# The mixers of the first block: the 16-row inverse moved ahead on VectorE, the convolution's input moved in front of it

## The chip, the cores and the metric

One core of a Trainium2 chip runs the whole program: two transformer-like blocks over 256 tokens of width 1024. Times are device microseconds (us) of one execution. The engines are TensorE (PE in the profile; its weight loads are PEld), VectorE (DVE), ScalarE (ACT), GpSimd (POOL) and SyncE (SP, which issues the weight loads). Each engine executes its instructions in a fixed order and waits on semaphores where an operand is not there yet.

## The reference, cut to what matters

The first block runs two layers; each has a mixer, then a feed-forward part (dense in the first layer, experts in the second). The change is in the mixer, which therefore runs twice. A mixer computes one input projection and three branches from it, and one output projection:

```python
proj = einsum('btd,de->bte', x, w_in)
(a_q, a_k, a_v, a_decay, a_beta, a_gate, c_glu, f_q, f_k, f_v, f_forget) = split_columns(proj, IN_SIZES)
# 1. gated delta rule, 6 heads of 64, chunks of 64 rows
qkv = silu(causal_depthwise_conv([a_q, a_k, a_v], gdn_conv_w))          # 4 taps
lower = where(strict, einsum('nbhcd,nbhsd->nbhcs', kb, kc) * decay, 0)
t_inv = triangular_solve(lower + eye, eye)                               # inverse of a 64 x 64 unit triangle
u, w = t_inv @ (vc * bc), t_inv @ (kb * exp(gc));  o_a = scan over 4 chunks, norm, gate
# 2. convolution
u = glu_a * sigmoid(glu_b);  u = causal_depthwise_conv(u, cnv_dw_w) + cnv_dw_b   # 31 taps, 256 channels
o_b = silu(layer_norm(u))
# 3. forgetting attention, 6 heads of 64, 256 tokens
o_c = softmax(q.k / 8 + decay, causal) @ v
mixed = [o_a, o_b, o_c] * mix_scale;  out = mixed @ w_out
```

## The kernel before, in words

The kernel is traced by one Python program (`Net.mixer1` for these mixers). The order in which statements are traced is their rank. A planner then lays every engine's instructions out in a fixed order ahead of time: whenever an engine is free in the planner's own timeline, the ready instruction of the best rank goes next, so an instruction of low rank fills a gap that one of high rank leaves while it is not ready. `with self.tc.issue_after(ins):` adds one more rule: what is traced inside it and runs on the engine of `ins` is placed behind `ins` on that engine. Only order is affected, and only that engine.

A projection is done in chunks of 256 columns, a 1 MB weight load each. `part` (L169 to L175) splits each half of a chunk into a rounded high part `wh` (ACT, L172) and the rest `wl` (DVE, L174), and `mm3` (L181) makes three matmuls of them, so a chunk is 48 matmuls of 128 x 128 by 256 columns and needs two ACT and two DVE instructions first. PSUM has two banks for projections (tag "a"), four for small work ("g") and two for the attention ("f").

The input projection has ten chunks in w_in_a (two tiles of 128 columns each, the last only one) and three in w_in_b. By `TILES_A`: chunks 0 to 2 are keys and queries of the delta rule, 3 the values v0 and v1, 4 v2 and f0, 5 f1 f2, 6 g0 g1, 7 g2 b0, 8 b1 a0, 9 a1, where f and g are the attention's keys and queries, b and a the two halves of the convolution's input.

A mixer is traced in this order (L624 to L636, L798):

- `pair_in`, `decays`, `pair_front` for chunks 0 to 2: 4-tap convolutions, norms, the triangles `NT`, and `lb`, the 16-row diagonal blocks of all twelve triangles.
- `spare(3)`, `spare(4)`: the values; `token_k`: keys by token.
- `emit(inverse(), scan(), fox(), conv(), gates())`, one after the other in rank. `inverse` begins with `invert16` (L503 to L513): 15 steps of a product (L509) and a reduction (L510) on DVE, each needing the one before, then a masking product (L511) and a 32 x 32 block transpose (L513). `invert32` goes from 16 to 64 rows by small matmuls, `solve` applies the inverse, `scan` carries the state over four chunks. `fox` projects chunks 5, 6, 7 and two of w_in_b, then does the attention for two blocks of 128 queries. `conv` projects chunks 8 and 9, gates the input into `up` (L748), does the last 6 (first mixer) or 8 (second) taps of each half of the channels with diagonal matrices on PE into one "a" bank (L757) and the other 25 or 23 one by one on DVE (L762, L764), adds both (L765) and normalises (L766 to L785). `gates` is the last chunk of w_in_b.
- the output projection, four chunks of w_out (L823).

Of the kernel before, what the change touches and what calls it, by code (L numbers as in the profile page):

```python
# [9 lines left out]
F32 = mybir.dt.float32  # L10
# [10 lines left out]
P = 128  # L21
D = 1024
KC = D // P
T = 256
# [53 lines left out]


TILES_A = "k0 q0 k1 q1 k2 q2 v0 v1 v2 f0 f1 f2 g0 g1 g2 b0 b1 a0 a1".split()  # L80
FOXC, GLUC = (5, 6, 7), (8, 9)

PCOLS1 = []
for _l in range(2):
# [19 lines left out]
class Net:  # L104
# [249 lines left out]
    def mixer1(self, l, x, xT):  # L354
        nc, A, ident = self.nc, self.A, self.ident
        V, S, PE = nc.vector, nc.scalar, nc.tensor
        wA, wB, wS = A["w_in_a"], A["w_in_b"], A["w_in_s"]
        mp = self.mp
        half = (slice(0, 64), slice(64, 128))

        def mm(out, lhsT, rhs, start=True, stop=True, **kw):
            PE.matmul(out, lhsT, rhs, start=bool(start), stop=bool(stop), skip_group_check=True, **kw)
# [28 lines left out]
        ps = self.ps("g", "cum").rearrange("p (t n) -> p t n", t=2)  # L391
# [68 lines left out]
        def pair_front(p):  # L460

            kq = kqs[p]
            sg = mp.tile([P, 2, T], F32, name="sg", bufs=3)
            S.activation(sg, kq, AF.Square)
            ps = self.ps("g", "l2")
            mm(ps, self.C["one64"], sg.rearrange("p a t -> p (a t)"))
            yield
            rs = mp.tile([P, 2, T], F32, name="sg", bufs=3)
            self.rsqrt(rs, ps.rearrange("p (a t) -> p a t", a=2), 1.0, 1e-6)
            V.tensor_tensor(kq, kq, rs, op=ALU.mult)  # L470
            yield
            at = AT[p] = mp.tile([P, 2, 2, 64], F32, name=f"AT{p}")
            nt = mp.tile([P, 2, 2, 64], F32, name=f"NT{p}")
            for o in range(2):
                e = E[2 * p + o]
                pk = self.ps("g", "kk")[:, :T].rearrange("p (t a n) -> p t a n", t=2, a=2)
                for t in range(2):
                    for c in range(2):
                        ts = slice(t * P + c * 64, t * P + c * 64 + 64)
                        mm(pk[half[c], t], kq[half[o], 0, ts], kq[half[o], :, ts])  # L480
                V.scalar_tensor_tensor(nt[:, o], pk[:, :, 0, :], -1.0, e[:, 1], op0=ALU.mult, op1=ALU.mult)
                V.scalar_tensor_tensor(at[:, o], pk[:, :, 1, :], 0.125, e[:, 0], op0=ALU.mult, op1=ALU.mult)
            n4 = NT[p] = nt.rearrange("p h t n -> p (h t) n")
            V.tensor_tensor(n4, n4, self.C["id64"][:, None, :].to_broadcast([P, 4, 64]), op=ALU.add)
            yield

            w = mp.tile([P, 4, 4, 16], F32, name="dgw")
            V.tensor_tensor(w, n4.rearrange("p i (b r) -> p i b r", b=4), self.C["in16"][:, None, :, None].to_broadcast([P, 4, 4, 16]), op=ALU.mult)
            d = mp.tile([P, 4, 16], F32, name="dg16", bufs=2)
            V.tensor_reduce(d, w.rearrange("p i b r -> p i r b"), axis=AX.X, op=ALU.add)  # L490
            yield
            for i in range(2):
                ex = mp.tile([P, 2, 16, 16], F32, name="sg", bufs=3)
                V.tensor_tensor(ex, d[:, 2 * i:2 * i + 2, :, None].to_broadcast([P, 2, 16, 16]),
                                self.C["id16"][:, None, None, :].to_broadcast([P, 2, 16, 16]), op=ALU.mult)
                pl = self.ps("g", "lb")
                mm(pl, self.C["one16"], ex.rearrange("p i r c -> p (i r c)"))
                S.activation(lb[:, 4 * p + 2 * i:4 * p + 2 * i + 2].rearrange("p i r c -> p (i r c)"), pl, AF.Copy)
            yield
# [3 lines left out]
        def invert16():  # L503

            xx = mp.tile([P, 12, 16], F32, name="x16")
            V.tensor_copy(xx, self.C["id16"][:, None, :].to_broadcast([P, 12, 16]))
            for r in range(1, 16):
                w = mp.tile([P, 12, 16], F32, name="w16", bufs=2)
                V.tensor_tensor(w[:, :, :r + 1], lb[:, :, r, :r + 1], xx[:, :, :r + 1], op=ALU.mult)  # L509
                V.tensor_reduce(xx[:, :, r], w[:, :, :r + 1], axis=AX.X, op=ALU.add)  # L510
            V.tensor_tensor(u32[:, 0].rearrange("p i (b r) -> p i b r", b=2), xx[:, :, None, :].to_broadcast([P, 12, 2, 16]),  # L511
                            self.C["even16"][:, None, :, None].to_broadcast([P, 12, 2, 16]), op=ALU.mult)
            V.transpose(u32[:, 1].rearrange("p i n -> p (i n)"), u32[:, 0].rearrange("p i n -> p (i n)"))  # L513

        def invert32(p):
            u, n4 = u32[:, :, 4 * p:4 * p + 4], NT[p]
# [95 lines left out]
        def spare(c):  # L612

            names = TILES_A[2 * c:2 * c + 2]
            ps = self.proj_a(wA[l, c][:, :1024 * len(names)], xT, tiles=len(names))
            for i, n in enumerate(names):
                if n[0] == "v":
                    value(ps[:, i, :], int(n[1]))
                else:
                    S.activation({"b": glu[:, 0:2], "a": glu[:, 2:4], "f": foxqk[:, 0:3], "g": foxqk[:, 3:6]}[n[0]][:, int(n[1]), :],  # L620
                                 ps[:, i, :], AF.Copy)
# [4 lines left out]
        for p in range(3):  # L626
            decays(p)
        self.weave(*(pair_front(p) for p in range(3)))
        spare(3)
        spare(4)  # L630
        for p in range(3):
            token_k(p)

        def fox():

# [50 lines left out]
                yield  # L686

        def inverse():
            invert16()
            yield  # L690
            self.weave(*(invert32(p) for p in range(3)))
            for p in range(3):
                solve(p)
                yield
# [42 lines left out]

        cv, csq = mp.tile([P, 2, T], F32, name="ccv"), glu[:, 0:2, :]

        def conv():  # L740

            for c in GLUC:
                spare(c)
            sg = glu[:, 0:2, :]
            self.sigmoid(sg, sg)
            up = mp.tile([P, 2, 30 + T], F32, name="cup")
            V.memset(up[:, :, 0:30], 0.0)
            V.tensor_tensor(up[:, :, 30:], glu[:, 2:4, :], sg, op=ALU.mult)  # L748
            yield
            near = 31 - (6, 8)[l]  # L750
            dw, db = self.col1(f"dww{l}"), self.col1(f"dwb{l}")
            pc = self.ps("a", "conv").rearrange("p (c n) -> p c n", c=2)
            for c in range(2):
                for j in range(near, 31):
                    dg = mp.tile([P, P], F32, name="dgt", bufs=2)
                    S.activation(dg, ident, AF.Copy, scale=dw[:, c * 31 + j:c * 31 + j + 1])
                    mm(pc[:, c, :], dg, up[:, c, j:j + T], start=j == near, stop=j == 30)  # L757
            for c in range(2):
                for j in range(near):
                    w = dw[:, c * 31 + j:c * 31 + j + 1]  # L760
                    if j == 0:
                        V.tensor_scalar(cv[:, c, :], up[:, c, 0:T], w, db[:, c:c + 1], op0=ALU.mult, op1=ALU.add)  # L762
                    else:
                        V.scalar_tensor_tensor(cv[:, c, :], up[:, c, j:j + T], w, cv[:, c, :], op0=ALU.mult, op1=ALU.add)  # L764
            V.tensor_tensor(cv, cv, pc, op=ALU.add)  # L765
            yield  # L766
            ps = self.ps("f", "cmean")
            for c in range(2):
                mm(ps[:, :T], self.ones, cv[:, c, :], start=c == 0, stop=c == 1)
            for c in range(2):  # L770
                V.scalar_tensor_tensor(cv[:, c, :], ps[:, :T], -1.0 / 256, cv[:, c, :], op0=ALU.mult, op1=ALU.add)
            S.activation(csq, cv, AF.Square)
            ps = self.ps("f", "cvar")
            for c in range(2):
                mm(ps[:, :T], self.ones, csq[:, c, :], start=c == 0, stop=c == 1)
            crs = glu[:, 2, :]
            self.rsqrt(crs, ps[:, :T], 1.0 / 256, 1e-5)
            lg_, lb_ = self.col1(f"clg{l}"), self.col1(f"clb{l}")
            for c in range(2):
                V.tensor_tensor(cv[:, c, :], cv[:, c, :], crs, op=ALU.mult)  # L780
                V.tensor_scalar(cv[:, c, :], cv[:, c, :], lg_[:, c:c + 1], lb_[:, c:c + 1], op0=ALU.mult, op1=ALU.add)
            V.tensor_scalar(csq, cv, -40.0, None, op0=ALU.max)
            self.sigmoid(csq, csq)
            V.tensor_tensor(cv, cv, csq, op=ALU.mult)
            yield  # L785
# [9 lines left out]
        msc = mp.tile([P, 8], F32, name="msc")  # L795
        V.tensor_copy(msc, self.col1(f"mix{l}"))
        V.tensor_scalar(msc[:, 0:3], msc[:, 0:3], self.col1(f"gnw{l}"), None, op0=ALU.mult)
        self.emit(inverse(), scan(), fox(), conv(), gates())  # L798
        mT = self.new_xT()
        for c in range(2):  # L800
            g = msc[:, 3 + c:4 + c]
# [1112 lines left out]
```

## Time and profile before

| | us |
|---|---|
| median of three timed runs (lowest, highest) | 2173.09 (2165.69, 2177.9) |
| the profiled execution | 2177.81 |
| its span | 2176.0 |
| PE busy in the span | 2079.3 |
| DVE busy | 1295.8 |
| ACT busy | 1017.1 |
| first mixer's output projection, last matmul | 203.0 |
| second mixer's | 608.6 |

The profile gives, for one execution, every instruction with its engine, line, tiles and times. A busy PE is modelled and includes matmuls at half clock, so the granted clock is read beside it. An engine's idle time stands in brackets behind the wait's releaser.

### The profile page before, as it was taken

How to read it: one execution, taken by the hardware profiler on the slowest of the kernel's cores; microseconds unless marked ns; L12 is line 12 of the kernel's file. 1: busy time of each engine (PE TensorE's matmuls, PEld its weight loads, DVE VectorE, ACT ScalarE, POOL GpSimd, SP SyncE). 2: the span in 40 equal slices, each digit the busy share in tenths (PEclk: the TensorE clock that was granted, in tenths of full speed). 3: DMA queues.
4: the chain of work that ended last, by engine and by line, in shares of the span. 5: the costliest groups of instructions: out<-in, count | busy, mean ns of one | idle time of the engine just before them, and what ended most of it. 6: DMA issues, size and time to landing. Idle time of an engine off the chain costs nothing. (4 is left out here: it accounts for less than half of the span.)

```text
span 2176.0 us, 31850 instructions
## 1 busy us (share of the span) xinstructions
PE 2079.3 (96%) x12770; PEld 1598.7 (73%) x12770; DVE 1295.8 (60%) x1903; ACT 1017.1 (47%) x1445; POOL 12.7 (1%) x27
## 2 busy tenths in 40 slices
PE   8998999899979999999999999999899999999998
PEld 7887999778766565565565565555699988888997
DVE  6767955676666555454564465454555568765444
ACT  6545444464435454444454454443444444644443
POOL 0000000000000000000000000000000000000000
PEclk9979999998889999999999999999999999999999
DMA  6313675422359999999999999999455553444552
GB/s 236 104 44 118 213 258 182 137 90 96 139 178 347 364 406 378 415 415 371 401 372 383 400 389 393 421 417 398 168 192 180 190 183 126 136 164 155 186 183 98
DMA packets 78987, 545.36 MB, mean 251 GB/s; under 512 B 8960, under 2 KB 11272, under 8 KB 13936
## 3 DMA queue, kind: packets, MB, share of 16 engines
q1 hardware_dynamic: 76112, 527.40, 63.8%
q0 software_dynamic: 2720, 15.84, 2.0%
q8 instruction: 103, 1.69, 0.3%
q14 instruction: 52, 0.43, 0.1%
HBM read 536.72 MB, written 6.49 MB: 250 GB/s over the span
## 5 line engine op out<-in xcount | busy, mean ns | idle before, releaser
L174 DVE TENSOR_TENSOR wl<-raw,wh 128x1024 fp32r<-128x1024 f32 (+1 forms) x662 | 798.1, 1217 | 432.3 <-ACT wh L172 420.5
L172 ACT ACTIVATE wh<-raw 128x1024 fp32r<-128x1024 f32 (+1 forms) x662 | 690.7, 1054 | 627.9 <-PE a_pA L184 270.3
L183 PE MATMUL a_pA<-xTh,wh 128*128 128x256 f32 x1456 | 419.0, 289 | 6.2 <-ACT foxqk L620 3.5
L185 PE MATMUL a_pA<-xTh,wl 128*128 128x256 f32 x1456 | 415.5, 286 | 0.8 <-DVE wl L174 0.7
L184 PE MATMUL a_pA<-xTl,wh 128*128 128x256 f32 x1456 | 415.6, 286 | 0.4 <-DVE xTl L278 0.2
L183 PEld LDWEIGHTS a_pA<-xTh,wh 128*128 128x128 f32 x1456 | 280.8, 193 | 14.7 <-ACT foxqk L620 5.6
L184 PEld LDWEIGHTS a_pA<-xTl,wh 128*128 128x128 f32 x1456 | 281.0, 193 | 5.3 <-issue 3.2
L185 PEld LDWEIGHTS a_pA<-xTh,wl 128*128 128x128 f32 x1456 | 280.8, 193 | 3.8 <-issue 2.2
L1033 PE MATMUL a_up<-raw,xef 128*64 128x512 f32 x896 | 213.5, 596 | 0.0
L184 PE MATMUL a_up<-wl,xeh 128*128 128x512 f32 x448 | 180.7, 403 | 0.5 <-DVE wl L174 0.4
L183 PE MATMUL a_up<-wh,xeh 128*128 128x512 f32 x448 | 177.7, 400 | 0.0
L185 PE MATMUL a_up<-wh,xel 128*128 128x512 f32 x448 | 177.3, 396 | 0.0
L1033 PEld LDWEIGHTS a_up<-raw,xef 128*64 128x64 f32 x896 | 65.1, 137 | 127.8 <-issue 122.3
L1038 DVE TENSOR_TENSOR mos<-mos,a_up 128x512 f32<-128x512 f32 x42 | 28.8, 685 | 200.3 <-PE a_up L1033 149.8
L183 PE MATMUL a_pB<-wh,xTh 128*128 128x256 f32 x480 | 141.5, 296 | 5.7 <-ACT glu L620 3.2
L185 PE MATMUL a_pB<-wh,xTl 128*128 128x256 f32 x480 | 138.6, 291 | 1.6 <-DVE xTl L278 1.6
L184 PE MATMUL a_pB<-wl,xTh 128*128 128x256 f32 x480 | 139.8, 292 | 0.0
L1066 PE MATMUL y_y<-raw,mof 128*64 128x512 f32 x448 | 132.8, 602 | 0.7 <-ACT mof L1052 0.7
L184 PEld LDWEIGHTS a_up<-wl,xeh 128*128 128x128 f32 x448 | 84.6, 189 | 34.5 <-issue 11.4
L183 PEld LDWEIGHTS a_up<-wh,xeh 128*128 128x128 f32 x448 | 84.7, 189 | 28.1 <-ACT wh L172 7.3
L185 PE MATMUL acc_acc<-wh,ffl 128*128 128x512 f32 x264 | 102.0, 392 | 0.0
L184 PE MATMUL acc_acc<-wl,ffh 128*128 128x512 f32 x264 | 101.9, 392 | 0.0
(556 smaller groups left out, 2703.2 us busy)
## 6 DMA issues: line engine op xcount, KB each, us to landing
raw<-in_moe_w_dram SPq DMA_DIRECT2D x336, 1024.0 KB, 9.2
raw<-in_ffn_in_dram SPq DMA_DIRECT2D x44, 1024.0 KB, 4.9
raw<-in_ffn_w_dram SPq DMA_DIRECT2D x33, 1024.0 KB, 5.0
raw<-in_w_in_a_dram SPq DMA_DIRECT2D x24, 1024.0 KB, 4.9
raw<-in_ffn_out_dram SPq DMA_DIRECT2D x22, 1024.0 KB, 4.9
raw<-in_w_out_dram SPq DMA_DIRECT2D x12, 1024.0 KB, 4.9
raw<-in_w_in_g_dram SPq DMA_DIRECT2D x12, 1024.0 KB, 4.9
raw<-in_w_in_b_dram SPq DMA_DIRECT2D x6, 1024.0 KB, 5.1
```

Source lines behind the costliest of these rows:

```text
L172: nc.scalar.activation(wh[:, :m], raw[:, o:o + m], AF.Copy)
L174: nc.vector.tensor_tensor(wl[:, :m], raw[:, o:o + m], wh[:, :m].bitcast(F32), op=ALU.subtract)
L183: mm(out, lh, rh, start=start, stop=False, skip_group_check=True)
L184: mm(out, lh, rl, start=False, stop=False, skip_group_check=True)
L185: mm(out, ll, rh, start=False, stop=stop, skip_group_check=True)
L1033: PE.matmul(ps[r], xe[0][:, k0, r], w[:, k * 512:k * 512 + 512], start=k0 == 0, stop=k0 == 7, skip_group_check=True)
L1038: V.tensor_tensor(s, s, pp[1], op=ALU.mult)
L1066: PE.matmul(py[h][r], hf[:, k, r], w[:, j * 1024 + h * 512:j * 1024 + h * 512 + 512], start=b == 0 and k == 0, stop=b == 6 and k == 3, ski ...
```

## The change

`invert16` is traced right after `pair_front`, ahead of the values' chunks and of token_k, and returns its last instruction, `solved`. Chunks 7, 8 and 9 are traced in front of the woven block, chunks 5 and 6 stay in the attention. The whole `emit` stands inside `issue_after(solved.ins)`. The convolution is cut in two: `conv_in` (gating and the diagonals on PE) comes behind the scan and ahead of the attention, the taps on DVE stay behind the attention. The convolution's mean and variance use a PSUM bank of tag "g" in place of "f".

```diff
-FOXC, GLUC = (5, 6, 7), (8, 9)
+GLUC, FOXC = (7, 8, 9), (5, 6)
...
-            V.transpose(u32[:, 1].rearrange("p i n -> p (i n)"), u32[:, 0].rearrange("p i n -> p (i n)"))
+            return V.transpose(u32[:, 1].rearrange("p i n -> p (i n)"), u32[:, 0].rearrange("p i n -> p (i n)"))
...
         self.weave(*(pair_front(p) for p in range(3)))
+        solved = invert16()
         spare(3)
         spare(4)
         for p in range(3):
             token_k(p)
+        for c in GLUC:
+            spare(c)
...
         def inverse():
-            invert16()
-            yield
             self.weave(*(invert32(p) for p in range(3)))
...
-        def conv():
-
-            for c in GLUC:
-                spare(c)
+        up = mp.tile([P, 2, 30 + T], F32, name="cup")
+
+        near = 31 - (6, 8)[l]
+        dw, db = self.col1(f"dww{l}"), self.col1(f"dwb{l}")
+        pc = self.ps("a", "conv").rearrange("p (c n) -> p c n", c=2)
+
+        def conv_in():
+
             sg = glu[:, 0:2, :]
             self.sigmoid(sg, sg)
-            up = mp.tile([P, 2, 30 + T], F32, name="cup")
             V.memset(up[:, :, 0:30], 0.0)
             V.tensor_tensor(up[:, :, 30:], glu[:, 2:4, :], sg, op=ALU.mult)
-            yield
...
                     dg = mp.tile([P, P], F32, name="dgt", bufs=2)
                     S.activation(dg, ident, AF.Copy, scale=dw[:, c * 31 + j:c * 31 + j + 1])
                     mm(pc[:, c, :], dg, up[:, c, j:j + T], start=j == near, stop=j == 30)
+            yield
+
+        def conv():
+
             for c in range(2):
                 for j in range(near):
...
-            ps = self.ps("f", "cmean")
+            ps = self.ps("g", "cmean")
...
-            ps = self.ps("f", "cvar")
+            ps = self.ps("g", "cvar")
...
-        self.emit(inverse(), scan(), fox(), conv(), gates())
+        with self.tc.issue_after(solved.ins):
+            self.emit(inverse(), scan(), conv_in(), fox(), conv(), gates())
```

## Rows read from the trace of the kernel before

**Rows 1.** The page's 40 slices of the span: PE's busy tenths, granted clock in tenths.

```profile
PE   8998999899979999999999999999899999999998
PEclk9979999998889999999999999999999999999999
```

**Rows 2.** Windows, first mixer: stretch and length, each engine's busy time, PEclk, DMA share, GB/s.

```profile
87.70:122.60 34.90, 34.85 (x485) 31.47 (x486) 25.87 (x67) 17.29 (x41) 0.00 (x0) 0.99 0.41 141
122.60:146.60 24.00, 24.00 (x187) 16.50 (x183) 12.50 (x38) 8.93 (x33) 0.00 (x0) 0.51 0.01 2
146.60:165.00 18.40, 18.32 (x180) 16.62 (x176) 15.70 (x36) 8.09 (x16) 0.00 (x0) 1.00 0.17 58
165.00:184.00 19.00, 13.84 (x80) 11.85 (x80) 14.33 (x36) 10.50 (x24) 2.06 (x4) 0.82 0.30 115
```

**Rows 3.** Windows, second mixer's stretch at half clock.

```profile
525.40:552.70 27.30, 27.30 (x210) 19.26 (x210) 14.00 (x41) 10.40 (x36) 0.00 (x0) 0.51 0.00 1
```

**Rows 4.** Timeline of PE, first mixer: start, duration, line, tiles, count, idle before.

```profile
87.75 0.39 PE L183 MATMUL a_pB<-wh,xTh 128*128 128x256 f32 x1 [1.58 <-ACT glu L620]
...
165.83 1.13 PE L362 MATMUL f_cmean<-ccv,ones 128*128 128x256 f32 x4 [0.81 <-DVE ccv L765]
...
174.49 0.66 PE L267 MATMUL g_tr<-call,mixed 128*128 128x128 f32 x4 [1.39 <-DVE mixed L816]
...
202.61 0.28 PE L184 MATMUL a_pB<-wl,xTh 128*128 128x256 f32 x1
202.73 0.28 PE L185 MATMUL a_pB<-wh,xTl 128*128 128x256 f32 x1
207.14 2.21 PE L869 MATMUL a_tr<-call,x 128*128 128x128 f32 x9 [4.13 <-DVE x L864]
```

**Rows 5.** Timeline of DVE, first mixer.

```profile
81.38 0.18 DVE L509 TENSOR_TENSOR w<-lb,x 128x24 f32<-128x24 f32 x1 [1.00 <-ACT lb L498]
...
88.98 0.26 DVE L509 TENSOR_TENSOR w<-lb,x 128x96 f32<-128x96 f32 x1
89.27 0.25 DVE L510 TENSOR_REDUCE x<-w 128x12 f32<-128x96 f32 x1
...
106.73 0.58 DVE L513 STREAM_TRANSPOSE u<-u 128x384 f32<-128x384 f32 x1
...
165.10 0.67 DVE L765 TENSOR_TENSOR ccv<-ccv,a_conv 128x512 f32<-128x512 f32 x1
```

**Rows 6.** Groups by line on DVE, 81.3 to 107.4 us.

```profile
L174 DVE TENSOR_TENSOR wl<-raw,wh 128x1024 fp32r<-128x1024 f32 x6 | 7.3, 1223 | 1.2 <-ACT wh L172 1.2
L509 DVE TENSOR_TENSOR w<-lb,x 128x24 f32<-128x24 f32 (+14 forms) x15 | 4.0, 268 | 1.2 <-ACT lb L498 1.0
L510 DVE TENSOR_REDUCE x<-w 128x12 f32<-128x24 f32 (+14 forms) x15 | 3.9, 262 | 0.2
...
L560 DVE TENSOR_TENSOR kbg<-g_ktok,ce 128x256 f32<-128x256 f32 x3 | 1.2, 414 | 0.0
```

**Rows 7.** Timeline of ACT: copies of chunk 6 and of chunk 7's gated half.

```profile
79.03 0.65 ACT L620 ACTIVATE foxqk<-a_pA 128x256 f32<-128x256 f32 x2
...
87.32 0.38 ACT L620 ACTIVATE glu<-a_pA 128x256 f32<-128x256 f32 x1
```

**Rows 8.** Windows: the start after PE's stop behind the first output projection.

```profile
207.10:211.10 4.00, 3.94 (x18) 3.58 (x18) 3.62 (x13) 2.57 (x6) 0.00 (x0) 0.57 0.00 0
```

**Rows 9.** Groups by line on DVE, 118 to 166 us: taps, and the attention's reductions.

```profile
L764 DVE SCALAR_TENSOR_TENSOR ccv<-cup,p,ccv 128x256 f32<-128x256 f32 x48 | 20.6, 476 | 0.2
...
L661 DVE TENSOR_REDUCE fsx<-f_fl 128x2 f32<-128x512 f32 (+1 forms) x4 | 2.2, 558 | 11.7 <-PE f_fl L362 11.7
```

**Rows 10.** Timeline of DVE, second mixer: the chain's first link and its transpose.

```profile
484.22 0.18 DVE L509 TENSOR_TENSOR w<-lb,x 128x24 f32<-128x24 f32 x1 [1.00 <-ACT lb L498]
...
509.57 0.58 DVE L513 STREAM_TRANSPOSE u<-u 128x384 f32<-128x384 f32 x1
```

**Rows 11.** Timeline of PE, second mixer: the output projection's last matmul.

```profile
608.33 0.28 PE L185 MATMUL a_pB<-wh,xTl 128*128 128x256 f32 x1
```

More of the change, by code (lines that the diff above doesn't have):

```diff
@@ L738, in mixer1 @@
         cv, csq = mp.tile([P, 2, T], F32, name="ccv"), glu[:, 0:2, :]
-        def conv():
-            for c in GLUC:
-                spare(c)
+        up = mp.tile([P, 2, 30 + T], F32, name="cup")
[3 more added lines that the diff above has]
+        def conv_in():
             sg = glu[:, 0:2, :]
             self.sigmoid(sg, sg)
-            up = mp.tile([P, 2, 30 + T], F32, name="cup")
             V.memset(up[:, :, 0:30], 0.0)
             V.tensor_tensor(up[:, :, 30:], glu[:, 2:4, :], sg, op=ALU.mult)
-            yield
-            near = 31 - (6, 8)[l]
-            dw, db = self.col1(f"dww{l}"), self.col1(f"dwb{l}")
-            pc = self.ps("a", "conv").rearrange("p (c n) -> p c n", c=2)
             for c in range(2):
```

## The prediction

> **What bounds the kernel now.** I read the page's slices first: TensorE (PE) is at 0.9 or above nearly everywhere, and its granted clock dips in the slices of the two mixers of the first block [rows 1]. Next, the windows of the first of them. From 87.7 to 165.0 us PE never stands still (34.85 of 34.90, 24.00 of 24.00 and 18.32 of 18.40 us busy), but from 122.6 to 146.6 it runs at 0.51, the lower level of 1.2 GHz [rows 2]. The second mixer does the same for 27.3 us [rows 3]. Then the timeline of PE: the output projection ends at 202.73 + 0.28 = 203.0 us [rows 4]. Its 4 x 48 matmuls follow each other every 0.12 us (two neighbours in [rows 4]), so it is worth 23.0 us and stands as if it had begun at 180.0. Between 165.0 and 180.0 lie only nine small pieces of PE work, from the 1.13 us of cmean to the 0.66 us of the last transposes, 7.0 us by their durations [rows 4]: 8 us of that tail are waits. Last, VectorE (DVE): the inverse's chain runs from 81.38 to 107.31 us [rows 5].
>
> So a mixer has three reserves: 12.0 us (half of 24.0) of lost clock, 8 us of waits in the tail, and whatever PE could do earlier. The profiled execution took 2177.81 us for a span of 2176.0; the median of the three timed runs is 2173.09, 4.7 less. I work with differences from the profiled one and subtract them from the median.
>
> **The change, part by part.**
>
> **1. The inverse is done earlier.** Its 15 products and 15 reductions last 4.0 and 3.9 us [rows 6]; alone, each follows 0.03 to 0.04 us after the end of the one before (89.27 after 88.98 + 0.26 [rows 5]), so 30 x 0.035 = 1.0 us is added, and 1.1 us for the masking product and the transpose (0.55 and 0.58): 10 us. It took 26, because weight splits (six of 1.22 us in that stretch), token work and the attention's reductions were placed between its links [rows 6]. Now everything of the woven block waits behind the transpose on DVE; what is still allowed between are operations traced before it: three products and three scalings of the values, three taps of v2, six of token_k (the splits of chunks 3 to 9 are through by then: chunk 9's one stands where chunk 7's first stood, at 79 us). These 15 cost about 0.41 us each, as token_k's [rows 6], but each fills a link's own gap, so I add 0.25 each: 3.5 us. The start stays at 81.38, since what feeds it is unchanged. Solved at 81.4 + 10 + 3.5 = 95.0 us; bounds 91.5 (nothing between) and 100 (all 15 in full, some beyond that). It was 107.3.
>
> **2. The price: PE has nothing to do meanwhile.** The splits of the attention's chunks are DVE work of the woven block, so they are queued behind the transpose too. ScalarE's halves are not, but PE needs both. Before, five chunks fed PE until it waited at 86.2 (1.58 us, released by the copy of the gated input [rows 4]): the v chunks 3 and 4, then 5 and 6 (6 copied out at 79.03) and 7 (its gated half at 87.32) [rows 7]. Now 7, 8, 9 stand in the place of 5, 6, 7, and chunk 9 has one tile: 24 x 0.12 = 2.9 us less work. PE is out of projections at 86.2 - 2.9 = 83.3 us and gets the next at 95. In between it has the transposes of v2 and k, 0.95 us (an estimate from their share around 94 us). About 11 us idle, where it was 1.5.
>
> After such a stop the clock is down: when PE had waited 4.13 us before 207.14, the next 4 us ran at 0.57 [rows 4, 8], a loss of 4.0 x 0.43 = 1.7 us. The Trainium skill, "TensorE: Matmul & The Clock Gate", section "Why this matters for your kernels", says to leave no idle gaps between bursts of matmuls, because the clock then falls to half; it speaks against this wait, and the row agrees. [...]
>
> **3. What then runs beside what.** After the transpose the small matmuls (three 32-row inverses, solve, scan, the convolution's diagonals) rank first, and five chunks of 5.8 us (chunks 5 and 6 and three of w_in_b) lie under them as filling. Before, four and a half of these lay ahead and only one was left beside the small work; there the engine did 18-, 32- and 64-row matmuls when the clock fell at 122.6. With dense 128-row chunks mixed in I expect most of the 12.0 us back. What is left is the end of the attention, which now comes after its late chunks with only w_in_b's last chunk beside it. Lost clock after the change: 4 us (1.7 at the restart, the rest there); bounds 0 and 14 (the clock stays down for another 24 us).
>
> **4. The convolution.** No instruction is added or removed: still 31 taps for each of two channel groups, on PE (the last 6 or 8 of each) and DVE. The input gating moves from the back to 95 us (the DVE product waits for the transpose), the diagonals follow. The first mixer's last 48 taps on DVE are 20.6 us, and DVE then sat idle 11.7 us in front of the attention's reductions with taps queued behind them [rows 9]. They ended so late that the sum of the two halves stood at 165.10 [rows 5], and the chain behind it (mean, variance, sigmoid, splits) held the output projection. Now the taps can start 25 us earlier; between 95 and 150 us DVE has about 30 us of other work (ten splits of 1.22 us [rows 6]; the inverse, scan and attention some 17, an estimate from the timeline) and 20 of taps, so the sum should come by 150 and the chain be covered. Waits left in the tail: 3 us, for the attention's last output and its transposes; bounds 0 and 8 (as now). The move of its mean to another PSUM tag is costed at nothing, since no wait of PE names a bank there.
>
> The diagonals' accumulator now holds one of two projection banks from 95 us until the sum. With one bank each chunk waits for its copy, 1.58 us in the row at 87.75 [rows 4], five times: 8 us if nothing else is ready. I take 0, because small work is: the half-clock stretch alone holds 12 us of it at full clock [rows 2], and the scan comes on top. 8 stays as a bound.
>
> DMA: the weight loads change their order on SP's queue, not their number; none is added on POOL's.
>
> **Sum for the first mixer**, in PE time at full clock: 165.0 - 87.7 = 77.3, less 12.0 of lost clock = 65.3; plus 2.9 (the tile that is now behind), less 0.95 done in the wait, plus 7.0 of the tail. 95.0 + 65.3 + 2.9 - 0.95 + 7.0 = 169.2, against 180.0: 10.8 us of room, minus 4 of clock and 3 of waits = 3.8 us gained. The second mixer's chain starts at 484.22 and ends at 510.15 [rows 10], the same 25.9 us; its output projection ends at 608.61 [rows 11]. Its half-clock stretch is 3.3 us longer, its tail about as much shorter, so I take the same: 7.6 in all. 2173.1 - 7.6 = **2166 us** (2170 for a profiled execution like this one). Its own range: 2158 to 2172.
>
> **The rivals.**
>
> A. *The tail and the clock come back whole.* For it: waits on DVE and half clock were each other's cause (a reduction waiting for a slow PE holds the taps [rows 9]). Then clock loss 1.7, waits 1: 10.8 - 2.7 = 8.1 a mixer, and 3.5 more if solved comes at 91.5; 16 to 23 in all, **2154**. Against it: the 11 us stop.
>
> B. *It does not do what it says:* wherever a chain link is not ready, the planner still puts something between, so solved comes at 100, PE stands 16 us, and what is gained behind is given back in front. Room 5.8, minus 4 and 3: -1.2 a mixer, **2175**.
>
> C. *The stop breaks the clock and the small work keeps it down.* One mechanism: PE stands idle from 83 us, restarts low, and what ranks first is the 32- and 64-row work that before the change ran 24 us at 0.51 [rows 2]. For it: exactly that work could not bring the clock back then. Against it: chunk 5 can enter as soon as its split of 1.22 us is done. Price: lost clock 12 + 1.7, waits 3: 10.8 - 16.7 = -6 a mixer, **2185**. It decides from about 8 us of lost clock a mixer, above which the kernel is slower than before.
>
> D. *One bank.* Four of the five copies are not covered, 6 us: 3.8 - 6 = -2.2 a mixer, **2177**. For it: the wait at 87.75, when chunk 4 held the other bank; against it: there no small work was ready.
>
> **How the numbers follow.** Forecast 0.42, A 0.20, B 0.13, C 0.17, D 0.08. About 0.5% (10.9 us) is what a measurement of this kernel can tell from no change. Faster by more: A and nearly two fifths of the forecast's case, 0.36. Within it: the rest of the forecast's, B and D, 0.44. Slower: C and a few of D, 0.20. The range for eight in ten runs from a little beyond A to C: 2149 to 2186.
>
> **What would show it.** Right: DVE's transpose (L513) near 95 and 498 us, with no weight split between the chain's links; PE's wait ahead of the first chunk after it about 11 us long; the granted clock near 1.0 from about 100 to 140 us; the convolution's sum (L765) before 155; the output projection of the first mixer ending near 199. Wrong: splits still between the links, or the transpose after 100 (B); a half-clock stretch of 15 us or more behind it (C); PE waiting on ACT copies at every chunk (D). Outside the mixers every stage should keep its length within 1 us; if time moves there, the forecast's ground is wrong.

## The result and the profile after

The changed kernel takes 2188.66 us (median of five, 2188.06 to 2188.87) against 2173.09 (2165.69 to 2177.9): ratio 1.0071, 95% interval 1.0049 to 1.0092. It is slower; 2166 was forecast. The profiled execution took 2188.06 us, its span is 2186.3.

Profile after, DVE's timeline in the first mixer: the chain's first link and its transpose, and the convolution's sum.

```profile
81.16 0.18 DVE L509 TENSOR_TENSOR w<-lb,x 128x24 f32<-128x24 f32 x1 [1.34 <-ACT lb L498]
...
94.87 0.58 DVE L513 STREAM_TRANSPOSE u<-u 128x384 f32<-128x384 f32 x1
...
128.47 0.69 DVE L769 TENSOR_TENSOR ccv<-ccv,a_conv 128x512 f32<-128x512 f32 x1
```

The inverse is there 11.9 us earlier and the sum 36.6 us earlier than in [rows 5]. In the second mixer the transpose starts at 504.23, where [rows 10] had 509.57, though that mixer began 6.2 us later. Beside the chain's links stand only values and keys, no weight split (groups on DVE, 81 to 95.5 us; columns as in [rows 6]):

```profile
L509 DVE TENSOR_TENSOR w<-lb,x 128x24 f32<-128x24 f32 (+14 forms) x15 | 4.0, 268 | 1.6 <-ACT lb L498 1.3
L510 DVE TENSOR_REDUCE x<-w 128x12 f32<-128x24 f32 (+14 forms) x15 | 4.0, 265 | 0.4
L425 DVE SCALAR_TENSOR_TENSOR v<-a_pA,p,v 128x255 f32<-128x255 f32 (+2 forms) x3 | 1.4, 479 | 0.0
L560 DVE TENSOR_TENSOR kbg<-g_ktok,ce 128x256 f32<-128x256 f32 x3 | 1.2, 414 | 0.0
...
```

PE's waits from 80 to 209 us (what waits, for what, us in total, times, longest):

```profile
PE g_x L362 <- DVE u L513: 7.3, 1, 7.3
PE g_vtok L573 <- DVE v L570: 3.1, 1, 3.1
PE f_fl L362 <- ACT fp L668: 2.5, 1, 2.5
PE f_fpt L677 <- ACT fpT L679: 1.5, 1, 1.5
PE a_pA L183 <- ACT glu L620: 0.9, 1, 0.9
PE a_conv L362 <- DVE cup L752: 0.9, 1, 0.9
PE f_fo L362 <- ACT fpT L679: 0.4, 1, 0.4
```

The first two, 10.4 us, are PE's stop ahead of the transpose. Windows of the first mixer, and of the second mixer's two low stretches (length, then busy PE, PEld, DVE, ACT, POOL; PEclk; DMA):

```profile
83.20:95.60 12.40, 1.97 (x14) 1.36 (x14) 11.37 (x39) 3.01 (x7) 0.00 (x0) 0.67 0.00 1
95.60:101.10 5.50, 4.60 (x107) 4.14 (x108) 5.44 (x10) 0.81 (x2) 0.00 (x0) 0.51 0.01 3
101.10:165.90 64.80, 62.81 (x724) 55.01 (x723) 44.98 (x106) 31.96 (x75) 0.00 (x0) 1.00 0.29 99
165.90:183.00 17.10, 14.61 (x48) 9.93 (x49) 9.84 (x26) 7.84 (x26) 0.53 (x1) 0.50 0.11 45
183.00:208.60 25.60, 25.60 (x217) 25.43 (x215) 16.33 (x29) 11.72 (x17) 1.54 (x3) 1.00 0.51 179
496.90:510.60 13.70, 5.30 (x111) 4.46 (x110) 13.19 (x34) 0.81 (x2) 0.00 (x0) 0.50 0.04 6
575.40:589.10 13.70, 12.78 (x37) 7.78 (x37) 8.54 (x24) 7.80 (x25) 0.54 (x1) 0.50 0.08 27
```

The 24.0 us at half clock of [rows 2] are gone: from 101.1 to 165.9 the clock is whole. In their place stand the stop with its restart, and 17.1 us at half clock at 165.9, where the attention's second half runs almost alone. Each mixer shows the same pair.

The two mixers as a whole, each up to the last matmul of its output projection; the kernel before, then after:

```profile
0.00:203.00 203.00, 186.59 (x1650) 162.12 (x1650) 140.30 (x331) 106.30 (x220) 4.54 (x12) 0.91 0.36 129
402.20:608.60 206.40, 187.10 (x1660) 160.17 (x1658) 140.89 (x320) 101.95 (x216) 0.53 (x1) 0.90 0.33 117
```

```profile
0.00:208.60 208.60, 182.32 (x1650) 158.50 (x1650) 139.81 (x330) 105.90 (x220) 4.55 (x12) 0.92 0.35 126
408.40:616.30 207.90, 180.61 (x1660) 156.71 (x1658) 142.87 (x321) 102.31 (x217) 0.54 (x1) 0.91 0.29 105
```

The number of matmuls is equal, so the fall in busy time is put down to the clock; the rest of the length is idle. Busy: 373.7 to 362.9 us, 10.8 won. Idle: 16.4 + 19.3 = 35.7 to 26.3 + 27.3 = 53.6, 17.9 lost. So the mixers are 7.1 us longer; 0.6 came between them and 2.6 behind them, 10.3 in the span. The other 5.3 of the 15.6 are scatter between executions: the profiled execution of before lay 4.7 above its median, that of after 0.6 below.

### The profile page after: what moved, and what is told of

It is laid out like the page before. It is cut to its first block, busy times and chain, and to the rows that moved or that the text cites. A ratio compares the mean times of both kernels' runs of the same rounds, so it can differ in the third digit from the quotient of the medians.

```text
span 2186.3 us, 31867 instructions
## 1 busy us (share of the span) xinstructions
PE 2072.6 (95%) x12770; PEld 1595.2 (73%) x12770; DVE 1297.5 (59%) x1903; ACT 1017.0 (47%) x1445; POOL 12.7 (1%) x27
```

## The experiments

The theory at the start: two separate losses in each mixer, (1) the stop, with its restart, and (2) the attention's late end at half clock. Rival 1: the stop is all of it. Rival 2: the convolution's early input and its bank.

All medians, with the ratio to runs of the kernel before on the same chip; from the profiled execution, PE idle and busy in the two mixers (windows as above), and the *edited stretches*: in each mixer the time from the chain's first link (L509) to the output projection's last matmul, both mixers added. Outside them the runs do the same work but for a few matmuls, and a median holds that part too.

| kernel | us | ratio, 95% interval | idle, busy | edited stretches |
|---|---|---|---|---|
| before | 2173.09 | | 35.7, 373.7 | 246.0 |
| changed | 2188.66 | 1.0071 [1.0049, 1.0092] | 53.6, 362.9 | 253.3 |
| e1 without the rule of order | 2199.44 | 1.0114 [1.0097, 1.0132] | 40.6, 385.0 | 261.5 |
| e4 convolution's part alone | 2200.46 | 1.0115 [1.0090, 1.0141] | 41.5, 392.4 | 267.1 |
| e5 inverse's part alone | 2238.0 | 1.0294 [1.0275, 1.0312] | 82.7, 390.5 | 318.9 |
| f1 one chunk in front | 2177.62 | 1.0015 [0.9999, 1.0032] | 45.5, 366.4 | 248.3 |
| e2 two: 5 and 6 | 2164.82 | 0.9954 [0.9939, 0.9969] | 31.9, 360.1 | 223.7 |
| e7 two of w_in_b | 2163.98 | 0.9951 [0.9933, 0.9970] | 36.0, 363.0 | 229.6 |
| f3 three | 2156.84 | 0.9925 [0.9900, 0.9950] | 30.8, 356.3 | 223.7 |
| f5 the same, run again | 2155.28 | 0.9905 [0.9882, 0.9927] | 30.6, 361.8 | 223.7 |
| e8 four | 2166.14 | 0.9965 [0.9946, 0.9983] | 33.0, 365.1 | 232.5 |
| f2 stop filled, unused work | 2182.24 | 1.0044 [1.0026, 1.0062] | 38.6, 383.2 | 255.7 |
| e3 unused work beside the scores | 2228.82 | 1.0255 [1.0227, 1.0284] | 67.3, 391.1 | 293.4 |
| e6 last chunk beside the scores | 2199.85 | 1.0117 [1.0083, 1.0152] | 54.4, 383.4 | 271.7 |
| e9 scores first | 2193.5 | 1.0102 [1.0076, 1.0128] | 58.4, 370.5 | 264.6 |
| b3 two in front, scores first | 2169.62 | 0.9992 [0.9978, 1.0006] | 36.4, 365.3 | 235.5 |
| e11 rule for the taps alone | 2181.55 | 1.0047 [1.0021, 1.0073] | 37.1, 373.4 | 243.5 |
| b4 that, scores first | 2194.19 | 1.0097 [1.0061, 1.0133] | 44.6, 378.2 | 257.6 |
| b2 two in front, no rule | 2165.34 | 0.9976 [0.9956, 0.9996] | 34.1, 366.5 | 232.6 |
| f4 three in front, no rule | 2171.7 | 0.9983 [0.9965, 1.0001] | 34.1, 372.7 | 243.8 |

Each run has one profiled execution. How far the rest moves by itself is seen in f3 and f5, which are one program: their edited stretches are equal, but the first chain begins at 78.83 us in f3 and at 84.06 in f5, whose clock was at 0.63 from 43.3 to 56.9 where f3's was whole.

**The parts apart: e1, e4, e5.**

```diff
-        with self.tc.issue_after(solved.ins):
-            self.emit(inverse(), scan(), conv_in(), fox(), conv(), gates())
+        self.emit(inverse(), scan(), conv_in(), fox(), conv(), gates())
```

> The changed kernel without the rule that puts everything of the woven block behind the inverse's transpose; the ranks stay as changed. The changed kernel takes 2188.7 us, the one before 2173.1. Theory: the loss has two places in each mixer, PE's stop of 11 to 12 us ahead of the transpose (with a restart at half clock, 2.7 us more), and the attention's second half, which now comes last and alone on PE at half clock (7 to 8 us). Without the rule the first place goes: PE's longest wait between 80 and 100 us falls below 4 us, the transpose comes later than 94.9 (97 to 106), the low stretch around the attention's end stays: 2172 to 2182. Rival 1, the stop is all of it: 2160 to 2168, faster than before. Rival 2, the cause is the convolution's input in front and the bank that its sums hold: no change, 2186 to 2191.

e4 is e1 with this besides; e5 is the kernel before with `solved = invert16()` behind `pair_front` and its own `emit` behind `solved`.

```diff
-        solved = invert16()
...
         def inverse():
+            invert16()
+            yield
```

> The convolution's part of the change alone: chunks 7, 8, 9 and the gated input in front, taps on DVE behind, its sum in another PSUM tag; the 16-row inverse is at its old place inside the woven block, with no rule for the order. Theory: no stop ahead of the transpose; the convolution's sum comes early, the attention's second half comes last and runs at half clock, 7 to 8 us lost there against 8 us of waits won: 2168 to 2178, about as before. Rival 1 (the stop is all of the loss): 2160 to 2168. Rival 2 (the convolution's part is the loss): 2184 to 2191.

> The inverse's part of the change alone: the kernel before with the 16-row inverse traced ahead of the values and the woven block behind its transpose; chunks and convolution as before. Theory: PE's stop ahead of the transpose is 6 to 10 us (the transpose at 93 to 96), the attention still comes ahead of the convolution's end, so its scores have dense chunks beside them: one place of loss, not two. 2174 to 2184. Rival 1 (the stop is all): 2184 to 2190, like the whole change. Rival 2 (the convolution's part is the loss): 2164 to 2175.

All three miss, and on the wrong side. Each costs more than the whole change, in the edited stretches too, so the loss can't be shared out between the parts. In e1 the groups on DVE from 80 to 122 us show why the transpose came at 121.25, 14.5 us later than in [rows 5]:

```profile
L768 DVE SCALAR_TENSOR_TENSOR ccv<-cup,p,ccv 128x256 f32<-128x256 f32 x42 | 18.5, 477 | 0.0
L174 DVE TENSOR_TENSOR wl<-raw,wh 128x1024 fp32r<-128x1024 f32 x8 | 9.7, 1217 | 2.9 <-ACT wh L172 2.9
```

The early input makes the 48 taps ready, and 42 of them filled the gaps of the chain. What came behind then ran almost without dense chunks, 28 of 353 matmuls (window of e1):

```profile
130.00:177.80 47.80, 47.80 (x353) 37.18 (x350) 13.46 (x37) 17.81 (x51) 0.00 (x0) 0.50 0.06 23
```

So the rule protects the chain from the early input's taps. The inverse's part without that input (e5) also has the stop, leaves all of chunks 5 to 9 behind the transpose, the convolution's last, and its sum comes at 200.92 us.

**The stop filled: e2, e7, e8, f1, f3.** All put chunks in front of the woven block, where they need not wait for the transpose.

```diff
-GLUC, FOXC = (7, 8, 9), (5, 6)
+GLUC, FOXC = (5, 6, 7, 8, 9), ()     # e2; f1: (5, 7, 8, 9), (6,)
```

> The changed kernel with the attention's chunks 5 and 6 also in front of the woven block, so that they need not wait for the transpose: 11.6 us of dense work that can fill PE's stop of 11 to 12 us. Theory (stop, and the attention's end at half clock): the stop goes almost whole and the attention's scores can begin earlier; what stands behind the transpose has 11.6 us less filling, so a new stretch at half clock is possible there. 2167 to 2176. Rival 1 (the stop is all): 2160 to 2168, and no other low stretch grows. Rival 2 (the held bank, the convolution's input): PE waits at the chunks for their copies, 2184 or more.

```diff
         for c in GLUC:
             spare(c)
+        ps = self.proj_b(wB[l, 0], xT)   # taken out of fox(); f3: this one, with e2's line
+        S.activation(fv[:, :, 0:256], ps, AF.Copy)
+        ps = self.proj_b(wB[l, 1], xT)   # e7: both; e8: both, with e2's line
...
```

> The changed kernel with two chunks of w_in_b, the attention's values, in front of the woven block, in place of the chunks 5 and 6 of the run that gave 2164.8. PE's stop is filled with as much dense work as there, but the attention's scores still have to wait for their own chunks behind the transpose. Theory (two places of loss: stop 10.4 us idle with its restart, and the attention's late second half at half clock): the first place goes, 10 to 12 us a mixer, the second stays or grows: 2166 to 2176. Rival (the earlier scores made that run's gain, the stop was harmless): 2184 to 2192. Rival (the stop was all of it): 2160 to 2166, as that run or below.

> Both pairs of chunks in front of the woven block, 5 and 6 and the attention's values: seven chunks and one of w_in_b's three is left as filling behind the transpose. Theory (dense work is a stock: 11 us of it are needed in the stop, and what is spent ahead is missing beside the 32- and 64-row matmuls): no stop, but a stretch of 14 us or more at half clock behind the transpose, as in the run without the rule of order (47.8 us): 2170 to 2188, slower than with two chunks less in front (2164.8). Rival (only the stop counts): 2158 to 2166.

> The changed kernel with chunk 5 alone in front of the woven block, half of what filled the stop in the run that gave 2164.8. Theory (the time follows the stop's length): 5.8 of 10.4 us idle go in each mixer, 2174 to 2180, half way between 2188.7 and 2164.8. Rival (what counts is that the clock falls in the stop, and it still falls in one of 5 us): 2184 or more. Rival (a stop of 5 us keeps the clock up): 2164 to 2170.

> Chunks 5, 6 and the first of the attention's value chunks in front of the woven block: 17.4 us of dense work for a stop of 10.4. Between the runs with two (2164.8, 2164.0) and four (2166.1): if the time follows the stop alone, 2162 to 2167 and no difference; if dense work ahead is missing behind, 2165 to 2170.

With 0, 1, 2, 3 chunks in front the medians are 2188.7, 2177.6, 2164.8 (or 2164.0) and 2156.8 us; a fourth gives 9 back. f1 came as its theory had it, e2 and e7 as the rival had it that the stop is all; e8 is 0.1 us outside its rival's range, f3 outside both of its ranges. The even steps of some 11 us, about twice a chunk's 5.8, are luck: in the edited stretches one chunk is worth 5 us, two are worth 24 (e7) or 30 (e2), a third nothing, and a fourth costs 9. PE's waits from 78 to 105 us say why the third is worth nothing. In f1 the wait for the transpose is still 6.3 us, but the 3.1 us in front of it are gone; in e2 there is no wait for the transpose any more, and a third chunk has nothing to fill (f1, then e2, then f3):

```profile
PE g_x L362 <- DVE u L513: 6.3, 1, 6.3
PE a_pA L183 <- ACT glu L620: 0.9, 1, 0.9
PE a_conv L362 <- DVE cup L752: 0.8, 1, 0.8
```

```profile
PE a_pA L183 <- ACT foxqk L620: 0.9, 1, 0.9
PE a_conv L362 <- DVE cup L752: 0.6, 1, 0.6
```

```profile
PE a_pA L183 <- ACT foxqk L620: 0.9, 1, 0.9
```

Windows of the edited stretches, of the changed kernel, of e2, of e7 and of f3:

```profile
81.16:208.63 127.47, 111.67 (x1119) 97.90 (x1118) 90.00 (x215) 57.34 (x130) 2.07 (x4) 0.88 0.27 92
490.52:616.35 125.83, 111.91 (x1128) 98.26 (x1126) 85.48 (x201) 55.59 (x128) 0.54 (x1) 0.89 0.28 105
```

```profile
80.59:191.59 111.00, 108.14 (x1119) 95.03 (x1118) 87.95 (x214) 56.63 (x130) 2.07 (x4) 0.95 0.30 106
478.69:591.36 112.67, 107.28 (x1127) 94.57 (x1126) 81.56 (x198) 53.21 (x127) 0.54 (x1) 0.98 0.38 138
```

```profile
81.58:200.04 118.46, 112.05 (x1119) 99.34 (x1118) 88.23 (x214) 57.46 (x130) 2.07 (x4) 0.91 0.29 99
487.07:598.20 111.13, 105.34 (x1127) 93.28 (x1126) 83.19 (x199) 55.10 (x128) 0.53 (x1) 1.00 0.36 133
```

```profile
78.83:191.63 112.80, 108.68 (x1120) 97.43 (x1118) 88.07 (x214) 57.46 (x130) 2.08 (x4) 0.92 0.30 104
475.62:586.50 110.88, 108.08 (x1127) 95.43 (x1126) 81.34 (x198) 54.16 (x127) 0.54 (x1) 0.97 0.38 140
```

From the changed kernel to e2 PE's idle time in them falls by 21.5 us, about as much as the two stops had (10.4 and 10.6), and its busy time by 8.1.

e7 and e2 have the same median, though the attention's last sum over the values ends at 178.6 in the one and at 165.5 in the other. In the first mixer that shows: e7's stretch is 118.5 us against 111.0. In the second e7's attention ends late as well (18.9 us ahead of the mixer's end, in e2 30.2), but its clock is whole, and its stretch is 111.1 against 112.7. So the stop's filling counts, which speaks for rival 1 (rival 2 asked for 2184 or more in e2 and falls); whether a late end is a loss of its own stays open. e8's 13.7 us at half clock behind the transpose (at 141.6) are what the stock theory asked for. By the medians they cost 1.3 us against e2, within the intervals; the edited stretches are 8.8 us longer.

None of f3's lead over e2 is in the edited stretches. Of 10.9 us between the two spans, 1.8 lie ahead of the first chain, 3.1 between the first mixer's end and the second chain, and 6 behind the mixers, in stages that no edit touched. f5 is f3 again and held: the 3.1 and the 6 came again. Why they are shorter with a third chunk stays open. What was expected of f5:

> The version with three chunks in front once more: 2152 to 2160 if its time holds; 2162 to 2168 if it was chance and the third chunk is worth nothing.

**Idle time or clock: f2.** 60 matmuls whose results go unused, in the stop.

```diff
+        pd = self.ps("g", "dense")
+        for i in range(60):
+            mm(pd[:, :T], xT[0][:, i % 8, 0:P], xT[0][:, i % 8, :])
```

> The changed kernel with 60 matmuls of 128 x 128 by 256 columns in each mixer's stop, behind the last projection and the key transposes, ahead of the first matmul that needs the inverse; their results go unused. 60 x 0.12 = 7.2 us, as long as the wait of 7.3 us for the transpose. It leaves the idle time lost and takes away only the clock's fall. Theory (the stop costs its idle time, 10.4 us a mixer, and 2.7 us of restart at half clock): only the restart comes back, 2181 to 2185. Rival (the clock's fall in the stop is the larger part and reaches on into the attention's late end): 2166 to 2178. Rival (nothing of it is clock): 2187 to 2190.

The median is as the theory had it, 6.4 us less for 5.4. From 95 to 105 us the clock is now whole (window of f2, then the changed kernel's):

```profile
95.00:105.00 10.00, 9.66 (x164) 9.26 (x162) 9.70 (x24) 1.21 (x3) 0.00 (x0) 1.00 0.11 20
```

```profile
95.00:105.00 10.00, 8.51 (x221) 7.62 (x222) 9.94 (x24) 1.61 (x4) 0.00 (x0) 0.70 0.34 108
```

But the 6.4 us are not where the theory had them. f2's edited stretches are 255.7 us, 2.4 longer than the changed kernel's:

```profile
83.85:212.31 128.46, 119.85 (x1179) 107.62 (x1178) 91.21 (x216) 57.41 (x130) 2.08 (x4) 0.89 0.27 92
493.75:621.00 127.25, 120.86 (x1187) 106.44 (x1186) 85.39 (x201) 55.39 (x128) 0.54 (x1) 0.92 0.30 110
```

They have 14.7 us less idle time and 17.1 more busy, 14.4 of it the added work (120 x 0.12): 2.7 are left over, so the clock won at the restart was lost again, and the first mixer's attention now ends with 20.4 us at 0.50 (from 169.2) in place of 17.1. The profiled execution, 4.2 us above f2's median, is 1.7 us faster than the changed kernel's, and that comes from behind the mixers: 1563.6 against 1570.0 us, in stages that no edit touched. So the stop's price is its time, as far as this run shows (3.1 us of each stop, the wait for the values, stayed); keeping the clock up through it won nothing in the mixers. The Trainium skill, "TensorE: Matmul & The Clock Gate", section "Why this matters for your kernels", asks for no idle gaps between bursts of matmuls; the two windows from 95 to 105 us agree with it, and the stretches show that following it for the clock's sake alone was worth nothing here.

**The attention's end: e3, e6, e9, b3.** Three ways to take the low stretch at 165.9 away, and one with the stop filled as well (`marks` is a list of the score matmuls, kept for these edits).

```diff
+                    if t:                                                # e3
+                        pd = self.ps("a", "dense")
+                        with self.tc.issue_after(marks[-1][2].ins):      # the group's last score matmul
+                            for i in range(10):
+                                mm(pd[:, :T], xT[0][:, i % 8, 0:P], xT[0][:, i % 8, :])
...
+            with self.tc.issue_after(first.ins):                         # e6; first: t=1's first score matmul
+                ps = self.proj_b(wB[l, 2], xT)
```

> The changed kernel with 40 matmuls of 128 x 128 by 256 columns added to each mixer, ten behind each of the four score groups of the attention's second half; their results go unused. They are 40 x 0.12 = 4.8 us of PE a mixer, 9.6 in all. Theory (the attention's second half is slow because the clock is at half there, and dense matmuls beside it would hold it): the low stretch of 17.1 us at 165.9 goes or shrinks to 7 or less, which gives back 5 to 8.5 us a mixer, about what the added work costs: 2182 to 2190. Rival (its length is set by what it waits for on DVE and ACT, the clock only shows it): the added work comes on top, 2194 to 2200.

> The changed kernel with the last chunk of w_in_b, 5.8 us of dense matmuls that ran ahead of the attention's second half, put behind that half's first score matmul; no work is added. Theory (half clock there for want of dense work): about half of the 17.1 us at the low level goes, 2 to 4 us a mixer: 2180 to 2185. Rival (the order of PE's own work is indifferent, its sum is what counts): 2187 to 2190. Rival (the chunk's own gating behind it is then last): 2190 to 2196.

In e9 the two `proj_b` of `fox` stand behind the scores of both halves, and each half has its own tile `fp`; b3 is e9 with e2's line.

> The changed kernel with the attention's order of rank altered: the scores and exponentials of both halves first, then the two chunks of w_in_b, then the transposes and sums over the values (the two halves' exponentials get a tile each). No work is added, and PE's stop ahead of the transpose stays as it is (10.4 us idle). Theory (two places: the stop, and the attention's second half that comes last at half clock): the second half's scores lie beside dense chunks, the low stretch of 17.1 us at 165.9 shrinks to 7 or less, the output projection ends 4 to 6 us earlier in each mixer: 2176 to 2182. Rival (only the stop counts; the runs with chunks moved into it gave 2164 to 2166 whether the attention's end was early or late): 2185 to 2190.

> The version with chunks 5 and 6 in front (2164.8) and the scores of both halves ahead of the chunks of w_in_b. If stop and attention's end are two separate losses, this one has neither: 2156 to 2163. If only the stop counts, or dense work that is spent beside the scores is missing beside the scan: 2163 to 2170.

All four miss their theory, b3 lies in its rival's range, and all are slower than without the edit: in the edited stretches 293.4, 271.7 and 264.6 us against 253.3, and 235.5 against e2's 223.7. In e6 the chunk was missing where it had been: the clock fell at 153.2 instead of 165.9, and 14 to 18 of its matmuls between the score groups did not bring it back. In e3 the added work pushed the same chunk behind the attention, and PE then waited 9.4 us for what is made of it, so that run is no clean test; there, too, the clock stayed down beside the added matmuls. In e9 the low stretches only changed places (6.8 us at 132.2, 13.7 at 176.6). Windows of e6 and of e3:

```profile
153.20:180.50 27.30, 27.25 (x96) 20.50 (x96) 8.48 (x25) 8.52 (x24) 0.00 (x0) 0.50 0.09 27
```

```profile
161.40:181.90 20.50, 20.50 (x77) 16.21 (x77) 4.32 (x14) 4.45 (x15) 0.00 (x0) 0.50 0.00 1
```

None of these ways took the second loss back by itself; that no other order does is not shown.

**What the rule is worth: e11, b4, b2, f4.** In e11 only `conv()` is emitted inside `issue_after(solved.ins)`; b4 is e11 with e9's order; b2 and f4 are e2 and f3 with e1's edit.

> The changed kernel with the rule of order kept for the convolution's taps alone: inverse, scan, convolution's input and attention may stand ahead of the transpose on DVE. Theory (what the rule must keep out is the 48 taps, which without it pushed the transpose to 121 us; what it should not keep out are the splits of the attention's chunks, for which PE stands still): transpose at 97 to 104, PE's wait below 3 us, 2162 to 2172. Rival (other work of the woven block, the gating and the scores' reductions, takes the gaps as the taps did): transpose after 108, 2176 or more.

> The rule kept for the taps alone, with the scores of both halves ahead of the chunks of w_in_b. If both hold (the rule's narrowing removes the stop, the earlier scores the attention's late end): 2154 to 2163. If the attention's order is indifferent: as the kernel with the narrowed rule alone, within 4 us.

> The version with chunks 5 and 6 in front, without the rule of order. Theory (the rule keeps the 48 taps of the convolution out of the inverse's gaps): transpose at 115 to 122 us as in the run without the rule (121), and with less dense work left beside what follows: 2185 to 2205. Rival (with the stop filled the rule does nothing): 2161 to 2168.

> The version with three chunks in front (2156.8), without the rule of order. If the rule's early transpose (97.9 us with it, 110 without it in the version with two chunks) is worth nothing while dense work lies ready: 2154 to 2160. If it is worth part of the 8 us that lay between two and three chunks: 2162 to 2168.

e11's transpose is at 98.38 and PE's wait for it is gone (idle 37.1), as expected; the time is not, 2181.55 with executions from 2172.71 to 2190.74: busy is 373.4 again, so the lost clock that the change had won is back. That the chunks which now run earlier are missing later would explain it, but was not tested by itself. b4 misses both its ranges: with the scores first it is 12.6 us slower than e11, as e9 and b3 are slower than the kernels they start from. In b2 the transpose is at 109.97, and the median is e2's, as the rival had it. The edited stretches differ: 232.6 us against 223.7. The rule is worth 9 us there, which the median hides, since behind the mixers b2 is 6 us shorter (1563.5, e2's 1569.4). f4 shows the need where a third chunk is in front: 15 us in the median, outside both its ranges, and 20 in the edited stretches. There the chain is late (110.57) and runs into this (window of f4):

```profile
130.00:160.70 30.70, 30.33 (x230) 23.02 (x229) 12.99 (x34) 12.33 (x35) 0.00 (x0) 0.50 0.01 1
```

## Why the prediction was wrong

The forecast's sign was wrong, and its sum (2165.5 before rounding) too low by 23 us: 9.4 and 5.3 in the two mixers, 3.2 between and behind them, and 5.3 that the two profiled executions lay off their medians (4.7 above, 0.6 below), which the sum had no term for.

- **Step 1, the inverse solved at 95.0:** 95.45. Right, with nothing but values and keys between its links (15 x 0.25 is 3.75 and not 3.5, which changes nothing). Rival B falls.
- **Step 2, the stop:** forecast 11 us, 10.4 measured; the restart at half clock cost 4.60 x 0.49 = 2.3 us of busy time up to 101.1 (1.7 forecast). Right. It was in the sum, as the start at 95.0.
- **Step 3 failed: "lost clock after the change: 4 us".** 2.3 at the restart and 14.61 x 0.50 = 7.3 at the attention's end make 9.6 us in the first mixer; in the second it is 5.30 x 0.50 and 12.78 x 0.50, 9.0. The step saw where the rest would lie ("only w_in_b's last chunk beside it") and mis-sized it: in the first mixer that chunk and the other two were through by 159.8 us, ahead of the second half's scores, and nothing dense was left beside them. The 12.0 us of [rows 2] were won and mostly given back at the two places. Rival C named the point of decision, 8 us of lost clock a mixer, and its 2185 was near, by luck: it did not name the place, since 5.5 us after the restart the clock was whole for 64.8 us, with the inverse's small matmuls in it.
- **Step 4, the convolution:** its sum came at 128.47, by 150 forecast. The tail's waits are the attention's now, 2.5 + 1.5 + 0.4 = 4.4 us, 3 forecast. Behind the transpose no chunk waits for a bank: rival D falls. PE's wait of 0.9 us for the gated input, at 98.0, was in no term (that for its copy, at 80.3, lies ahead of the stop).

The tail of [rows 4] was misread as well. Of its 8 us, 5.2 were waits. The output projection began at 175.88 and not at 180.0, and for 6.9 us it ran at 0.51, some 3 us of lost clock (timeline of PE and window, before):

```profile
175.88 0.39 PE L183 MATMUL a_pB<-wh,xTh 128*128 128x256 f32 x1 [0.73 <-ACT xTh L277]
```

```profile
176.80:183.70 6.90, 6.42 (x29) 6.28 (x30) 4.61 (x15) 3.14 (x6) 0.29 (x1) 0.51 0.73 297
```

For the first mixer: 208.6 less 23.0 for the output projection is 185.6; forecast 169.2 + 4 + 3 = 176.2. Of the 9.4 us between, 8.4 are found: 5.6 are the lost clock, 1.4 the tail, 0.9 the short wait, 0.5 the start. In the second, 206.4 less 3.8 was forecast and 207.9 measured; 5.0 of the 5.3 us are the lost clock. The text's own sign of a wrong ground, a stage outside the mixers that moves by more than 1 us, came as well: behind them 2.6 us were added.

What the runs showed in the place of step 3: 2.3 to 2.7 us of clock lost at the restart and 6.4 to 7.3 at the attention's end in each mixer, where 4 in all was forecast. Why the clock falls at the attention's end, and which dense work would have had to lie where, stays open: three attempts at it lost time, and in e7's second mixer a late end ran at whole clock. What can be won back is the stop, which the sum had paid for out of 10.8 us of room: with two chunks in it the edited stretches went from 253.3 to 223.7 us, and the median from 2188.7 to 2164.8.

## What to carry to other kernels

When a chain on one engine is put ahead of everything, count what the other engines can do until it ends, and place that much independent work in front of the barrier: here two chunks of 5.8 us in a stop of 10.4 us a mixer took 24 us off the median. Past a full stop more is not better: in the stretches that the edits change a third chunk brought nothing and a fourth cost 9 us, with a new stretch at half clock behind the barrier. So the number of pieces is to be measured, and moving one to where the clock is seen low can pull the fall forward (e6).

Read a gain where the edit acts, and not from the median alone: stages that no edit touched moved by up to 8 us, which stands for f2's gain and for half of the first chunk's, and hid what b2 and e8 lost. A rule of order and an earlier input were each harmful alone; test such parts together with what fills their waits.

## What the hardware showed that was not expected

The clock falls with PE continuously busy: 47.80 of 47.80 us at 0.50 (e1), 20.50 of 20.50 with unused dense matmuls among the scores (e3). After a stop of 12.4 us with 1.97 us of work it was whole again 5.5 us after the restart. And stages that no edit touched differ between the programs: from the second mixer's output projection to the end, 1567.4 us before, 1570.0 after, 1562.5 in e6, and 1563.4 in both f3 and f5, which are one program.
